# Attention weights times v: the first v tile loaded as 64 partitions of heads, and the next-to-last store cut into 112, 11 and 5 rows

## The chip, the core and the metric

The kernel runs on one core of a Trainium2 chip. The metric is the device time of one execution in microseconds (us). The kernel before was timed three times: 1051.83 us in the median, 1051.76 at the lowest and 1052.38 at the highest.

## What is computed

The reference is one contraction, for 8 batches of 12 heads. Inputs and output are float32.

```python
batch, n_heads, seq, head_dim = 8, 12, 1024, 64
# attn_weights: [8, 12, 1024, 1024], v: [8, 12, 1024, 64]
np.einsum('bhqs,bhsd->bhqd', attn_weights, v)
```

The weights are 402.65 MB, v and the output 25.17 MB each, so 453 MB have to cross between HBM and the core.

## The kernel before

**Tiles.** The 96 heads are taken four at a time: 24 groups q, each in two units n (48 units). A unit's weights are one transfer (`load_attn`, L346) of 128 partitions (four heads, 32 partitions each), 64 KB read and 32 KB written per partition, because this transfer also turns float32 into bf16. Two buffers `abf` take turns. The last two units are loaded in two halves each.

**Compute.** For each unit TensorE transposes the weights (L146); VectorE and ScalarE copy the result out of PSUM into `at` (L276). For the first unit of a group TensorE also spreads the group's v from `vr` over all partitions (L163) and two engines copy it to `vbf` (L252). Then it multiplies (L191). The product is copied to `ot` (L288), transposed back in the next unit (L176), and copied to `osb` (L259), the output buffer of ten slots. Each unit's transposes done, GpSimd (POOL) issues the load of the unit after next into the buffer that came free: the order on POOL is written out by hand in the loop `for n in range(NU - 2)`.

**v.** From group 2 on, v comes as bf16 through POOL's queue into `vr` (`load_v`, L352). The first two groups (8 heads) take another way. SyncE (SP) loads them as float32 into two slots of `osb` that are not yet used, called `v32` (128 partitions of 16 KB: 16 partitions per head, so partitions 0 to 63 hold group 0 and partitions 64 to 127 group 1). The 16 KB are loaded as two halves of the columns: the first 8 KB of all 128 partitions before the main section starts (L136, 1 MB), the second 8 KB as the first transfer in it (L413, 1 MB, `V_REST`). VectorE casts the first half to `vr` in two copies (L334), POOL the second (L393). `s_vr` tells TensorE that v is there: POOL's cast raises it by 2, for both groups, after waiting on `s_v0` for the second transfer and for VectorE's copies. The main section is entered by VectorE, ScalarE and SP once the first transfer has landed; POOL issues the first two weight loads ahead of that.

**Stores.** Outputs of groups 0 to 19 are stored by POOL's queue, in bursts of 2 to 8 groups (L360). The last four groups go by SP's queue: groups 20 and 21 in one transfer of 2 MB, group 22 in one of 1 MB (both through `store`, L360, behind SP's wait for the second half of the last weights, L430), and group 23 in one of 1 MB at the very end (L436). ScalarE waits for the three with `s_end`.

Two queues are told apart in the profile: q0, POOL's, with the weight loads, later v and most stores; and q1, SP's, with the first v and the last stores. Both feed the same 16 DMA engines; a transfer of 128 rows puts 8 rows on each.

Of the kernel before, what the change touches and what calls it, by code (L numbers as in the profile page):

```python
# [10 lines left out]
def kernel(  # L11
# [18 lines left out]
    nc = tc.nc  # L30
# [4 lines left out]
    B, H, Q, S = attn_weights.shape  # L35
    D = v.shape[-1]
    NH = B * H
    P = 128
# [4 lines left out]
    HP = P // 2  # L43
    KW = S // (2 * P)
    SB = S // P
    V8 = 2 * VH
    VB = S // (P // V8) // SB
    VR = 32
    NV = NH // VH
# [8 lines left out]
    V_SLOT = 4  # L58
    V_AT_ONCE = 4
    V_LOADS = {2: 2, **{q: V_AT_ONCE for q in range(V_AT_ONCE, NV, V_AT_ONCE)}}  # L60

    V_REST = ((0, P),)
    HALVED = NU - 2
    TOGETHER = 8
    BURSTS = {8: ((0, 8),), 16: ((8, 2), (10, 6))}
# [3 lines left out]
    def slot(q):  # L69
        return q % NO  # L70

    attn_q = attn_weights.rearrange("b (hq four) (p r) s -> (b hq) (four p) (r s)", four=VH, p=VP)
    out_q = out.rearrange("b (hq four) (p r) d -> (b hq) (four p) (r d)", four=VH, p=VP)
    out_h = out.rearrange("b h q d -> (b h) q d")

    def out_n(q, fours):
        return out_h[ds(q * VH, fours * VH)].rearrange(
            "(n four) (p r) d -> (four p) n (r d)", four=VH, p=VP
        )
# [3 lines left out]
    def v_n(q, fours):  # L83
        return v_h[ds(q * VH, fours * VH)].rearrange(
            "(n eight) (p r) d -> (eight p) n (r d)", eight=V8, p=P // V8
        )
# [17 lines left out]
    vr = sb("vr", [P, V_AT_ONCE // 2, VB, SB * D], bf16)  # L104
    vbf = sb("vbf", [P, SB, VH, D], bf16)
    ot = sb("ot", [P, GH, P], fp32)
    osb = sb("osb", [P, NO, 2 * G, D], fp32)

    v32 = osb[:, ds(V_SLOT, 2)].rearrange("p n r d -> p n (r d)")
    v_first = v_n(0, 2)[:, 0].rearrange("p (half x) -> p half x", half=2)  # L110
    vr_first = vr[:, 0].rearrange("p (half b) x -> p half (b x)", half=2)
    bank = [nc.alloc_psum_tensor(f"bank{i}", [P, 512], fp32).ap() for i in range(8)]
    pt = [b.rearrange("p (k j) -> p k j", k=KW) for b in bank[:4]]
    po = bank[4:6]
# [5 lines left out]
    s_v0, s_v = sem("s_v0"), sem("s_v")  # L120
    s_osb = sem("s_osb")
    s_held, s_end = sem("s_held"), sem("s_end")
# [8 lines left out]
    s_out, s_fin = sem("s_out"), sem("s_fin")  # L131
    s_const, s_vr = sem("s_const"), sem("s_vr")

    s_half, s_free = sem("s_half"), sem("s_free")

    nc.sync.dma_start(out=v32[:, 0], in_=v_first[:, 0])  # L136

    with tc.tile_critical(sync_engine=mybir.EngineType.Pool, no_gpsimd_drain=True):
        pe = nc.tensor
# [189 lines left out]

        for h in range(2):  # L330
            nc.vector.memset(ot[:, :, ds(h * HP, HP)], 0.0).then_inc(s_ot)
        for half in range(2):
            part = ds(half * (SB * D * VB // 4), SB * D * VB // 4)
            last = nc.vector.tensor_copy(out=vr_first[:, 0, part], in_=v32[:, 0, part])  # L334
        last.then_inc(s_v0)
        engine(True)
        engine(False)
        nc.scalar.wait_ge(s_held, 16 * (BY_SYNC - HELD_FROM) // 2)
# [2 lines left out]
        pool = nc.gpsimd  # L341

        def load_attn(n):
            pieces = [(0, G)] if n < HALVED else [(0, GH), (GH, GH)]
            for g0, gn in pieces:
                pool.dma_start(  # L346
                    out=abf[n % 2][:, ds(g0, gn)].rearrange("p g s -> p (g s)"),
                    in_=attn_q[n // 2][:, ds((n % 2 * G + g0) * S, gn * S)],
                ).then_inc(s_abf[n % 2] if g0 == 0 else s_second[n], 16)

        def load_v(q, fours):
            pool.dma_start(  # L352
                out=vr[:, ds(q % V_AT_ONCE // 2, fours // 2)].rearrange("p n b x -> p n (b x)"),
                in_=v_n(q, fours),
            ).then_inc(s_v, 16)

        def store(q, fours, eng, done):
            eng.wait_ge(s_out, 2 * (q + fours) + 1)
            at_slot = osb[:, ds(slot(q), fours)].rearrange("p n r d -> p n (r d)")
            eng.dma_start(  # L360
                out=out_n(q, fours), in_=at_slot,
                **({"single_packet": True} if eng is pool and fours == 2 else {}),
            ).then_inc(done, 16)

        def store_2(q):
# [7 lines left out]
            out=ident,  # L373
            in_=ident,
# [9 lines left out]
            out=spread,  # L384
            in_=spread,
# [3 lines left out]
            pattern=[[-P, V8], [-1, P + VB - 1]],  # L389
            channel_multiplier=VB,  # L390
        ).then_inc(s_const)
        pool.wait_ge(s_v0, 16 * len(V_REST) + 1)
        pool.tensor_copy(out=vr_first[:, 1], in_=v32[:, 1]).then_inc(s_vr, 2)  # L393
        for n in range(NU - 2):
            q, i = n // 2, n % 2
            if i == 0 and q + 1 in V_LOADS:
                pool.wait_ge(s_sp, 4 * (q + 1))
                load_v(q + 1, V_LOADS[q + 1])
            pool.wait_ge(s_t[True], (n + 1) * PER_DVE)
            load_attn(n + 2)  # L400
            if i == 0 and q % TOGETHER == 0 and 0 < q <= HELD_FROM:
                for q0, fours in BURSTS[q]:
                    store(q0, fours, pool, s_osb)
# [5 lines left out]

        for p0, pn in V_REST:
            nc.sync.dma_start(  # L413
                out=v32[ds(p0, pn), 1], in_=v_first[ds(p0, pn), 1]
            ).then_inc(s_v0, 16)
        nc.sync.sem_inc(s_free, NO // 2)
        nc.sync.sem_inc(s_half, WHOLE[0])
        for k in range(1, NV // 2):
# [9 lines left out]
        for n in range(HALVED, NU):  # L428
# [1 line left out]
            nc.sync.sem_inc(s_half)  # L430
        nc.sync.wait_ge(s_osb, 16 * sum(len(x) for x in BURSTS.values()))
        store(NV - 4, 2, nc.sync, s_end)
        store(NV - 2, 1, nc.sync, s_end)
        nc.sync.wait_ge(s_fin, 2)
        nc.sync.wait_ge(s_out, NU)
        nc.sync.dma_start(  # L436
            out=out_q[NV - 1], in_=osb[:, slot(NV - 1)].rearrange("p r d -> p (r d)")
        ).then_inc(s_end, 16)
        landed = nc.scalar.alloc_register("landed")
        nc.scalar.reg_mov(landed, 16 * 3)  # L440
    tc.keep_in_program_order(nc.scalar.wait_ge(s_end, nc.scalar.snap(landed)))
    tc.keep_in_program_order(nc.scalar.sem_inc(s_end, 1))

# [29 lines left out]
```

## Time and profile before

| | |
|---|---|
| time of the profiled execution | 1051.83 us |
| its span, first to last instruction | 1050.0 us |
| TensorE (PE) busy | 795.4 us, 76% of the span |
| VectorE (DVE) busy | 388.7 us, 37% |
| ScalarE (ACT) busy | 410.6 us, 39% |
| POOL busy | 39.1 us, 4% |
| moved in HBM | 427.82 MB read, 25.17 MB written |
| packets of q1 in the trace, 8,192 B each | 309 ns in the median |
| packets of a weight load on q0, 32,768 B written | 2,432 ns in the median |
| a weight load, from issue to landing | 29.2 us in the median |

The profile counts bytes of a DMA at its destination, so a weight load of 8 MB in HBM is 4,096 KB there. Its rate of 229 GB/s in the mean is therefore about half of what is read, while the last line of its third part gives the rate in HBM, 431 GB/s over the span. The line "DMA" of its second part is the busy share of the 16 DMA engines in 40 slices of the span. The trace also has a record of each packet that a DMA engine moved (start, length, size, queue); the same packets strung together by their ends give the work of each of the 16 engines. Times within the span are counted from its start.

### The profile page before, as it was taken

The numbers are of one execution on the slowest core, as the hardware profiler recorded it, in microseconds if no ns is written. First come the engines' busy times: TensorE is split into PE (matmuls) and PEld (weight loads), VectorE is DVE, ScalarE is ACT, GpSimd is POOL, SyncE is SP. The second block draws the span as 40 slices with busy tenths as digits, with TensorE's granted clock in tenths as the row PEclk, the third lists the DMA queues.
The fourth block names the chain that finished last, engine by engine and source line by source line (L and its number), as shares of the span: only waits on it lengthen the run. The fifth ranks groups of instructions, "written<-read, shape, count | busy, mean of one in ns | idle before, by whom it ended". The sixth has DMA issues, their size and how long they took to land.

```text
span 1050.0 us, 17183 instructions
## 1 busy us (share of the span) xinstructions
PE 795.4 (76%) x7304; PEld 708.4 (67%) x7304; DVE 388.7 (37%) x583; ACT 410.6 (39%) x493; POOL 39.1 (4%) x68
## 2 busy tenths in 40 slices
PE   0878789489789492887949779859568975887995
PEld 0777678478678482777848678647547865776885
DVE  1443344235334251343424344324223432453443
ACT  0444344335335251343425344334224433444443
POOL 1000000000000000000000000000000000000000
PEclk9989889799898796889879989889878988899898
DMA  9999999999999999999999999999999999999999
GB/s 232 229 218 219 217 216 212 217 220 218 217 218 216 212 216 379 217 218 217 207 218 220 220 218 217 207 224 212 324 275 217 218 206 220 217 220 220 209 218 352
DMA packets 12198, 240.20 MB, mean 229 GB/s; under 512 B 1056, under 2 KB 1056, under 8 KB 1056
## 3 DMA queue, kind: packets, MB, share of 16 engines
q0 software_dynamic: 11344, 233.84, 99.1%
q1 hardware_dynamic: 848, 6.29, 1.5%
q8 instruction: 3, 0.05, 0.0%
q14 instruction: 3, 0.02, 0.0%
HBM read 427.82 MB, written 25.17 MB: 431 GB/s over the span
## 4 chain that ended last, share of the span: by engine, by line
DMA 71%; PE 26%; issue 1%; POOL 0%; ACT 0%; DVE 0%; ACTq 0%; SPq 0%; POOLq 0%
DMA abf<-in_attn_weights_dram 63%; PE bank L146 22%; DMA out_dram<-osb 8%; PE bank L163 3%; PE bank L191 1%; PE bank L176 1%; POOL vr L352 0%; ACT vbf L252 0%; ACT osb L259 0%; DVE osb L259 0%; ACT ot L288 0%; POOL abf L346 0%; ACTq L259 0%; SPq L424 0%; SPq L423 0%
## 5 line engine op out<-in xcount | busy, mean ns | idle before, releaser
L146 PE MATMUL bank<-ident,abf 128*128 128x128 f32 x3072 | 430.0, 307 | 215.3 <-DMA abf<-in_attn_weights_dram 188.2
L146 PEld LDWEIGHTS bank<-ident,abf 128*128 128x128 f32 x3072 | 420.4, 212 | 227.1 <-DMA abf<-in_attn_weights_dram 195.6
L276 DVE COPY at<-bank 128x1024 bf16<-128x1024 bf16 x480 | 319.7, 689 | 405.1 <-PE bank L146 400.6
L276 ACT COPY at<-bank 128x1024 bf16<-128x1024 bf16 x288 | 287.9, 1012 | 332.0 <-PE bank L146 332.0
L191 PE MATMUL bank<-at,vbf 128*64 128x256 bf16 x3072 | 225.7, 285 | 0.0
L191 PEld LDWEIGHTS bank<-at,vbf 128*64 128x64 bf16 x3072 | 203.7, 111 | 19.4 <-issue 6.3
L288 DVE COPY ot<-bank 128x512 f32<-128x512 f32 x48 | 33.2, 692 | 208.6 <-PE bank L191 208.6
L288 ACT COPY ot<-bank 128x512 f32<-128x512 f32 x48 | 28.1, 585 | 185.9 <-PE bank L191 185.9
L163 PE MATMUL bank<-vr,spread 32*128 32x512 bf16 x768 | 87.0, 375 | 0.6 <-issue 0.2
L176 PE MATMUL bank<-ident,ot 128*128 128x128 f32 x392 | 62.4, 312 | 29.4 <-ACT vbf L252 28.7
L176 PEld LDWEIGHTS bank<-ident,ot 128*128 128x128 f32 x392 | 51.3, 159 | 41.4 <-ACT vbf L252 40.5
L259 ACT COPY osb<-bank 128x512 f32 (+1 forms) x97 | 53.4, 588 | 31.2 <-PE bank L176 29.3
L163 PEld LDWEIGHTS bank<-vr,spread 32*128 32x128 bf16 x768 | 35.2, 93 | 44.0 <-issue 1.7
L346 POOL DMA_DIRECT2D abf<-in_attn_weights_dram x50 | 26.9, 538 | 788.7 <-PE bank L146 787.7
L252 ACT CAST vbf<-bank 128x512 bf16<-128x512 f32 x48 | 25.8, 589 | 74.4 <-PE bank L163 74.4
L252 DVE CAST vbf<-bank 128x512 bf16<-128x512 f32 x48 | 30.9, 686 | 29.1 <-PE bank L163 29.1
L276 ACT ACT_TABLE_LOAD x12 | 15.4, 1283 | 6.7 <-DMA osb<-in_v_dram 6.5
L352 POOL DMA_DIRECT2D vr<-in_v_dram x6 | 4.0, 674 | 136.3 <-PE bank L163 136.3
L360 POOL DMA_DIRECT2D out_dram<-osb x5 | 3.9, 786 | 12.0 <-ACT osb L259 12.0
L393 POOL CAST vr<-osb 128x2048 bf16<-128x2048 f32 x1 | 1.9, 1889 | 22.0 <-DMA osb<-in_v_dram 22.0
L327 DVE MEMSET ident<- 128x128 f32 x1 | 0.2, 165 | 6.5 <-DMA osb<-in_v_dram 6.5
L334 DVE CAST vr<-osb 128x1024 bf16<-128x1024 f32 x2 | 2.2, 1138 | 0.0
(9 smaller groups left out, 5.3 us busy)
## 6 DMA issues: line engine op xcount, KB each, us to landing
abf<-in_attn_weights_dram POOLq DMA_DIRECT2D x46, 4096.0 KB, 29.2
vr<-in_v_dram POOLq DMA_DIRECT2D x5, 2048.0 KB, 15.3
out_dram<-osb POOLq DMA_DIRECT2D x1, 8192.0 KB, 41.7
abf<-in_attn_weights_dram POOLq DMA_DIRECT2D x4, 2048.0 KB, 23.0
out_dram<-osb POOLq DMA_DIRECT2D x3, 2048.0 KB, 33.4
out_dram<-osb POOLq DMA_DIRECT2D x1, 6144.0 KB, 41.7
osb<-in_v_dram SPq DMA_DIRECT2D x2, 1024.0 KB, 15.7
out_dram<-osb SPq DMA_DIRECT2D x1, 2048.0 KB, 14.4
```

Source lines behind the costliest of these rows:

```text
L146: last = pe.matmul(out=pt[g % 4][:, k], lhsT=words[:, k], rhs=ident, is_transpose=True, start=(k == 0), stop=(k == KW - 1),)
L163: last = pe.matmul(out=banks[h], lhsT=spread[rows, j, ds(VB - 1 - b, P)], rhs=vr[rows, n // 2, b], start=(b == 0), stop=(b == VB - 1),)
L176: last = pe.matmul(out=ps[:, ds(j * P, P)], lhsT=ot[:, j0 + j], rhs=ident, is_transpose=True, start=(j == 0), stop=(j == jn - 1),)
L191: last = pe.matmul(out=outs, lhsT=vbf[:, 2 * kw + par, h], rhs=at[:, ds(half * GH, GH), kw, ds(h * VP, VP), par], start=(n == 0), stop=(n ...
L252: copy(out=vbf[:, :, h], in_=ps.rearrange("p (k d) -> p k d", k=SB)).then_inc(s_vbf)
L259: return copy(out=rows.rearrange("p (half j) d -> p j half d", half=2)[:, ds(j0, jn)], in_=ps[:, ds(0, jn * P)].rearrange("p (j half d) -> ...
L276: ins = copy(out=at[:, g].rearrange("c k j two -> c (k j two)"), in_=bank[g % 4].bitcast(bf16),)
L288: copy(out=ot.rearrange("c j (h p) -> c h j p", h=VH)[:, ds(2 * e, 2)], in_=po[e].rearrange("c (h j p) -> c h j p", h=2, j=GH),).then_inc( ...
L334: last = nc.vector.tensor_copy(out=vr_first[:, 0, part], in_=v32[:, 0, part])
L346: pool.dma_start(out=abf[n % 2][:, ds(g0, gn)].rearrange("p g s -> p (g s)"), in_=attn_q[n // 2][:, ds((n % 2 * G + g0) * S, gn * S)],).th ...
L352: pool.dma_start(out=vr[:, ds(q % V_AT_ONCE // 2, fours // 2)].rearrange("p n b x -> p n (b x)"), in_=v_n(q, fours),).then_inc(s_v, 16)
L360: eng.dma_start(out=out_n(q, fours), in_=at_slot, **({"single_packet": True} if eng is pool and fours == 2 else {}),).then_inc(done, 16)
```

## The change

The first two groups' v is now split by partitions and not by columns. What is loaded before the main section is group 0 alone: partitions 0 to 63, 16 KB each, as two transfers of 64 x 8 KB (0.5 MB each). Group 1 (partitions 64 to 127) follows as one transfer of 64 x 16 KB in place of L413. VectorE casts group 0 in two copies of 64 x 2,048 elements and raises `s_vr` itself; POOL casts group 1 in one copy of 64 x 4,096 elements, and does so behind the issue of unit 2's weight load, no longer ahead of the loop. On SP the store of group 22 becomes three transfers, of rows 0 to 111, 112 to 122 and 123 to 127; ScalarE's last wait counts two transfers more. All bytes moved are the same as before.

```diff
-    V_REST = ((0, P),)
+    UNEVEN = ((0, 112), (112, 11), (123, 5))
...
+    four = [ds(0, HP), ds(HP, HP)]
+    VC = S * V8 * D // P // 2
+    part = [ds(0, VC), ds(VC, VC)]
...
-    nc.sync.dma_start(out=v32[:, 0], in_=v_first[:, 0])
+    for x in part:
+        nc.sync.dma_start(out=v32[four[0], x], in_=v_first[four[0], x])
...
-        for half in range(2):
-            part = ds(half * (SB * D * VB // 4), SB * D * VB // 4)
-            last = nc.vector.tensor_copy(out=vr_first[:, 0, part], in_=v32[:, 0, part])
-        last.then_inc(s_v0)
+        for x in part:
+            last = nc.vector.tensor_copy(out=vr_first[four[0], x], in_=v32[four[0], x])
+        last.then_inc(s_vr)
...
-        pool.wait_ge(s_v0, 16 * len(V_REST) + 1)
-        pool.tensor_copy(out=vr_first[:, 1], in_=v32[:, 1]).then_inc(s_vr, 2)
         for n in range(NU - 2):
...
             load_attn(n + 2)
+            if n == 0:
+                pool.wait_ge(s_v0, 16)
+                pool.tensor_copy(out=vr_first[four[1]], in_=v32[four[1]]).then_inc(s_vr)
...
-        for p0, pn in V_REST:
-            nc.sync.dma_start(
-                out=v32[ds(p0, pn), 1], in_=v_first[ds(p0, pn), 1]
-            ).then_inc(s_v0, 16)
+        nc.sync.dma_start(out=v32[four[1]], in_=v_first[four[1]]).then_inc(s_v0, 16)
...
-        store(NV - 2, 1, nc.sync, s_end)
+        nc.sync.wait_ge(s_out, 2 * (NV - 1) + 1)
+        for p0, pn in UNEVEN:
+            nc.sync.dma_start(
+                out=out_q[NV - 2, ds(p0, pn)],
+                in_=osb[ds(p0, pn), slot(NV - 2)].rearrange("p r d -> p (r d)"),
+            ).then_inc(s_end, 16)
...
-        nc.scalar.reg_mov(landed, 16 * 3)
+        nc.scalar.reg_mov(landed, 16 * (2 + len(UNEVEN)))
```

More of the change, by code (lines that the diff above doesn't have):

```diff
@@ L107 @@
     osb = sb("osb", [P, NO, 2 * G, D], fp32)
-    v32 = osb[:, ds(V_SLOT, 2)].rearrange("p n r d -> p n (r d)")
-    v_first = v_n(0, 2)[:, 0].rearrange("p (half x) -> p half x", half=2)
-    vr_first = vr[:, 0].rearrange("p (half b) x -> p half (b x)", half=2)
+    v32 = osb[:, ds(V_SLOT, 2)].rearrange("p n r d -> p (n r d)")
+    v_first = v_n(0, 2)[:, 0]
+    vr_first = vr[:, 0].rearrange("p b x -> p (b x)")
+    four = [ds(0, HP), ds(HP, HP)]
+    VC = S * V8 * D // P // 2
+    part = [ds(0, VC), ds(VC, VC)]
     bank = [nc.alloc_psum_tensor(f"bank{i}", [P, 512], fp32).ap() for i in range(8)]
```

## The prediction

> **What bounds the kernel now.** I read the page's parts 2 and 3 first. The line "DMA" is full in all 40 slices, and one queue alone fills 99.1% of the 16 DMA engines' time:
>
> ```profile
> span 1050.0 us, 17183 instructions
> ...
> PE 795.4 (76%) x7304; PEld 708.4 (67%) x7304; DVE 388.7 (37%) x583; ACT 410.6 (39%) x493; POOL 39.1 (4%) x68
> ...
> DMA  9999999999999999999999999999999999999999
> ...
> q0 software_dynamic: 11344, 233.84, 99.1%
> q1 hardware_dynamic: 848, 6.29, 1.5%
> ```
>
> TensorE, the busiest engine, works 76%. The chain of waits agrees: 71% of it is DMA, and its pieces alternate between a weight load's transfer and the 64 transposes that free the buffer for the load after next. Then the packet records: strung together, they give 16 DMA engines that carry packets from 1.85 us on, with no gap of 0.5 us or more on any, until they end between 1047.5 and 1048.7 us; the instructions end 1.3 us later. So the time is a sum of packets, and the engine with the longest sum ends it. No wait between compute engines matters unless it leaves a DMA engine without packets, and a loss on a DMA engine passes to the end in full. Two loads are always under way: when one's successor is issued, the other load still has about half of its 8 x 2.43 = 19.5 us of packets to run. The sum is made against the profiled execution, 1051.83 us, which is also the median of the three runs (span 1050.0 and 1.83 us around it).
>
> The start, from the timeline:
>
> ```profile
> 0.74 0.38 SPq L136 DMA_DIRECT2D osb<-in_v_dram  x1
> 1.34 1.23 POOL L346 DMA_DIRECT2D abf<-in_attn_weights_dram  x2 [0.90 <-POOLq L457]
> 6.33 0.33 SPq L413 DMA_DIRECT2D osb<-in_v_dram  x1
> ...
> 8.77 2.19 DVE L334 CAST vr<-osb 128x1024 bf16<-128x1024 f32 x2
> 27.68 9.12 PEld L146 LDWEIGHTS bank<-ident,abf 128*128 128x128 f32 x64 [27.68 <-DMA abf<-in_attn_weights_dram]
> ...
> 32.41 1.89 POOL L393 CAST vr<-osb 128x2048 bf16<-128x2048 f32 x1 [22.00 <-DMA osb<-in_v_dram]
> ```
>
> The reader is to see that the first transfer of v is ahead of everything on the DMA engines, and that the compute engines have nothing to do before 27.68 us but small preparations.
>
> **Casts: 0.** VectorE's two copies double in elements per partition: 2 x 2.19 = 4.4 us for 2.19, done by about 15.5 us even when they start 2 us later; VectorE's next work waits for the transposes at 27.68 us. POOL's cast likewise grows from 1.89 to 3.8 us, and stands behind the issue of unit 2's load (37.30 us). What is queued behind it is the issue of unit 3's load, 35 us later; the next to need its data is TensorE's spread at 77.11 us. `s_vr` for group 0 comes at 15.5 instead of 34.3 us, where TensorE uses it at 37.23 us: the wait there was not binding. If the cover were gone, VectorE's 2.2 us would only move copies of unit 0, which sets no DMA engine idle.
>
> **The first v: +2.05 us.** Before, each of the 16 engines moves 8 packets of 8,192 B. All but the first packets take 309 ns, one every 306; the first take 316 to 1,685. The engines finish between 4.79 and 5.83 us, in the mean at 5.05, and on all 16 the first load packet starts 5 to 6 ns behind the last record of v. The loads wait behind v on each engine. The number of bytes stays. But they now land in 64 partitions, 16 x 8,192 B per 306 ns, or 428 GB/s, into half as many rows. The trace shows no such transfer. The ends: nothing, if the 306 ns are the engine's own; or 8 x 309 ns = 2.47 us, if 64 partitions take only half of what 128 do. I take the ceiling that has been seen: 428 GB/s for 128 partitions, thus 214 GB/s for 64. It is the fastest that any partition receives in this trace; the weight loads write half as fast (32,768 B in 2,432 ns). Then 1,048,576 B take 4.90 us; from about 2.2 us, when the first packets are through, that ends at 7.1, against 5.05 in the mean: +2.05 us (part of the slow first packets is hidden, since engines that share rows wait for one another anyway).
>
> [...]
>
> **The second v: +0.8 us.** Before, its 8 packets of 322 ns per engine take turns with load packets of 2.43 us. After, 4 packets of 16,384 B do. At the engines' pace they take 4 x 0.62 us, the same work. Bounds: 0, and 4 x 0.62 = 2.48 us if each packet takes double. On average the upper 64 partitions need, per turn of 2.43 + 0.62 = 3.05 us, 8 x 32,768 B of load and 16 x 16,384 B of v, 172 GB/s, which is below the 214. So only coincidences cost: an engine that sends v to rows that another is filling with weights. I take a third of the upper end, 0.8 us. If the ceiling doesn't exist, this is 0.
>
> **The cut store: 0, bounds -0.31 and +0.31 us.** The 16 engines end at 1047.47 to 1047.98 us (eleven) and at 1048.24 to 1048.72 (five). With 112 rows as 7 on each engine, 11 rows on eleven and 5 on five, five engines carry 9 rows, six 8 and five 7, where all had 8; a packet is 306 ns. If the five late ones are the relieved, the end moves to 1048.41, -0.31; if one of the late is among the five with 9, +0.31. The records don't say which engine is which, so I take 0. The two more issues on SP (0.45 us each by the first two, 0.96 us in all for two) end by 1031.4 us; engines take up q1 at 1033.07 or later, and SP's next issue is at 1041.34 us.
>
> ```profile
> 1029.49 0.96 SPq L360 DMA_DIRECT2D out_dram<-osb  x2
> ...
> 1041.34 0.33 SPq L436 DMA_DIRECT2D out_dram<-osb  x1
> ```
>
> **Sum.** 1051.83 + 2.05 + 0.8 + 0 = 1054.7 us.
>
> **Rivals.**
> 1. *No ceiling in the partitions; not slower.* 64 partitions take 428 GB/s. Decided by the pace of a v packet in the first 6 us: 309 ns, and not near 618. For it: the engines move about 8 KB in 304 to 309 ns whether they write 8 KB into the core, 4 KB (cast loads) or read from it, as if the limit were in the engine. Against: no partition has been seen to take more than in that transfer. Then only the cut store is left: 1051.8 us, 1051.4 to 1052.2.
> 2. *Load packets fill the gaps.* If an engine takes a load packet in between as soon as POOL's descriptors are there, the slow v costs only until then: about half of 2.05, 1052.8 us, with some of the second v 1053.3. For it: later the two queues do take turns, packet by packet (10 to 32 us, and again from 1033 us). Against: at the start none of the 16 engines did; all 8 v packets went ahead, though the loads were issued at 1.34 us.
> 3. *The second v collides fully.* 2.05 + 2.48: 1056.4 us. For it: half the engines send into rows that others fill, and the last engine ends the kernel. Against: the mean need of 172 GB/s fits.
> 4. *The 11 and 5 rows all go to one engine.* It would carry 7 + 16 = 23 rows instead of 8: 15 x 0.306 = 4.6 us, if everything else is nothing 1056.4 us. Nothing in the trace has an odd number of rows. [...]
>
> **How the numbers follow.** Forecast (first v at half pace, second partly) 0.42, with its own range 1053.6 to 1055.7; rival 1 0.27; rival 2 0.13; rival 3 0.12; rival 4 0.04; something that saves over 2.1 us 0.02, for which I find no source: the engines' ends lie 1.25 us apart, and that is all that better balance could give. The range 1051.5 to 1056.3 leaves out the lowest part of rival 1, about half of rivals 3 and 4, and the last case, some 0.15 together. What a measurement of this kernel can tell from no change is about 0.2%, 2.1 us: slower means above 1053.9. That takes nine tenths of the forecast, rivals 3 and 4 and a little of rival 2: 0.56. Within: 0.42. Faster: 0.02.
>
> **What would show it.** In the profile after: the first v lands at about 8 us instead of 6.2 (SP's second issue moves from 6.33 to about 8.3 us), its packets last near 618 ns, and the first load packets start near 7 us. The second v's packets last 0.62 us without collisions and up to 1.24 with. PE's first transposes move from 27.68 to about 30 us, and everything behind them by the same 2 to 3 us up to the last store's issue, 1041.34 us before. In the tail the engines carry 7, 8 or 9 rows of group 22. If v's first packets still take 309 ns, the main step is wrong and rival 1 holds; if load packets lie between them, rival 2; if one engine ends some 4 us behind the others, rival 4.

## The result and the profile after

The changed kernel takes 1055.44 us in the median of 8 runs (1053.92 to 1059.22), the kernel before 1051.85 (1051.73 to 1052.38): a ratio of 1.0038, 95% interval 1.0028 to 1.0047. It is slower by 3.6 us, clear of what the measurement can tell, and its executions differ from one another by 5 us where those of before differ by 0.7. The profiled execution took 1056.10 us (span 1054.3). The forecast was 1054.7 us, slower, with 1051.5 to 1056.3 as the range; the time lies inside it, but two of the terms that it was added up from were far off, as the parts below show.

Parts 1 to 3 of the page after, the span and the queues (packets, MB, share of the time of 16 DMA engines):

```profile
span 1054.3 us, 17185 instructions
...
DMA  9999999999999999999999999999999999999998
...
q0 software_dynamic: 11344, 233.84, 98.7%
q1 hardware_dynamic: 816, 6.29, 1.7%
```

The DMA engines are as full as before. q1 moves the same 6.29 MB, but its packets take 1.7% of the engines' time and not 1.5%, and that of a longer span; by the packet records 18.4 us per engine instead of 15.5. The work of the engines has become longer, with the same bytes.

The timeline of the start (start, busy us, engine and line, and in brackets the idle time before it and what ended it), and behind it how long the two transfers of group 0 took from issue to landing:

```profile
0.74 1.18 SPq L140 DMA_DIRECT2D osb<-in_v_dram  x2
1.34 1.24 POOL L349 DMA_DIRECT2D abf<-in_attn_weights_dram  x2 [0.90 <-POOLq L463]
19.07 0.47 SPq L416 DMA_DIRECT2D osb<-in_v_dram  x1
19.22 0.17 DVE L331 MEMSET ident<- 128x128 f32 x1 [19.22 <-DMA osb<-in_v_dram]
...
21.52 3.25 DVE L337 CAST vr<-osb 64x2048 bf16<-64x2048 f32 x2
29.18 10.10 PEld L150 LDWEIGHTS bank<-ident,abf 128*128 128x128 f32 x64 [29.18 <-DMA abf<-in_attn_weights_dram]
...
39.77 0.57 POOL L349 DMA_DIRECT2D abf<-in_attn_weights_dram  x1 [16.08 <-PE bank L150]
40.39 3.59 POOL L404 CAST vr<-osb 64x4096 bf16<-64x4096 f32 x1
...
L140 SPq DMA_DIRECT2D osb<-in_v_dram x2: 549/562/575, 0.7 to 1.3; - x2
...
DMA to landing us min/median/max: 5.5/11.5/17.5
```

Three things are to be seen. The main section is entered at 19 us, not at 6.3: the second of the two transfers of group 0, issued at 1.3 us, takes 17.5 us to land. TensorE starts at 29.18 us, 1.5 later than before. And the casts still have cover: VectorE's end at 24.8 us, ahead of the spread (L167) at 39.71, and POOL's at 44.0, ahead of the next group's spread at 81.12.

The packet records say where the 1.5 us come from, and that it doesn't end there. One DMA engine of each kernel (start in us, 0.05 more here than counted from the first instruction; packet lengths in ns; v packets of 8 KB, or 16 KB where marked):

```
before  v 1.85+864, then seven of 309; load 4.85+2431, 7.26+2432, 9.68+2435; v 12.09+322; load 12.41+2431; ...
after   v 2.15+820 2.97+311 3.27+618 3.88+654; load 4.52+2526; v 7.03+322; load 7.35+2431; v 9.76+322; ...
        v 25.19+1052 (16 KB) 26.24+1649 (16 KB); load 27.88+2431; v 30.29+1058 (16 KB); load 31.32+2492;
        v 33.79+1064 (16 KB); ...
```

The records don't name their engine; which packets stand on the same one is inferred from starts that meet ends. All 16 engines together, in us per engine beyond the regular length (306 ns per 8 KB of v, 2,432 per load packet):

```
                              before   after   difference
first v, start of first packet  2.08    2.35     0.27
first v, packets too long       0.51    1.11     0.60
second v, packets too long      0.12    2.26     2.14
load packets beside them        0.04    0.50     0.46
sum                                              3.47
second load lands, mean        46.39   49.81     3.42
second load lands, last engine 47.46   51.91     4.45
last packet, last engine     1048.72 1053.02     4.30
```

From the second load's landing to the last weight load the mean delay stays between 3.2 and 3.5 us: nothing is lost or regained in 980 us, and what the start lost arrives at the end. The table is of one execution, which took 1056.10 us and is one of the longer ones. At the tail SP's issues moved by 4.4 us:

```profile
1033.85 0.42 SPq L363 DMA_DIRECT2D out_dram<-osb  x1
1034.33 2.21 SPq L436 DMA_DIRECT2D out_dram<-osb  x3
1045.71 0.36 SPq L442 DMA_DIRECT2D out_dram<-osb  x1
```

### The profile page after: what moved, and what is told of

It is laid out like the page before. It is cut to its first block, busy times and chain, and to the rows that moved or that the text cites. A ratio compares the mean times of both kernels' runs of the same rounds, so it can differ in the third digit from the quotient of the medians.

```text
span 1054.3 us, 17185 instructions
## 1 busy us (share of the span) xinstructions
PE 794.3 (75%) x7304; PEld 708.1 (67%) x7304; DVE 389.9 (37%) x583; ACT 410.6 (39%) x493; POOL 41.4 (4%) x68
## 3 DMA queue, kind: packets, MB, share of 16 engines
q1 hardware_dynamic: 816, 6.29, 1.7%
## 4 chain that ended last, share of the span: by engine, by line
DMA 71%; PE 26%; issue 1%; POOL 0%; ACT 0%; DVE 0%; ACTq 0%; SPq 0%; POOLq 0%
DMA abf<-in_attn_weights_dram 63%; PE bank L150 22%; DMA out_dram<-osb 8%; PE bank L167 3%; PE bank L195 1%; PE bank L180 1%; POOL vr L355 0%; ACT vbf L256 0%; ACT osb L263 0%; DVE osb L263 0%; ACT ot L292 0%; POOL abf L349 0%; ACTq L263 0%; SPq L425 0%; SPq L424 0%
## 5 line engine op out<-in xcount | busy, mean ns | idle before, releaser
L167 PE MATMUL bank<-vr,spread 32*128 32x512 bf16 x768 | 87.0, 375 | 0.5 <-issue 0.2
L167 PEld LDWEIGHTS bank<-vr,spread 32*128 32x128 bf16 x768 | 35.0, 93 | 44.1 <-issue 1.7
L404 POOL CAST vr<-osb 64x4096 bf16<-64x4096 f32 x1 | 3.6, 3591 | 0.1
L337 DVE CAST vr<-osb 64x2048 bf16<-64x2048 f32 x2 | 3.2, 1662 | 0.0
```

The source lines that it names most:

```text
L167: last = pe.matmul(out=banks[h], lhsT=spread[rows, j, ds(VB - 1 - b, P)], rhs=vr[rows, n // 2, b], start=(b == 0), stop=(b == VB - 1),)
L404: pool.tensor_copy(out=vr_first[four[1]], in_=v32[four[1]]).then_inc(s_vr)
```

## The experiments

Theories are named in the expectations as they stood: **A**, engines that write v into 64 partitions at once get half the rate, in the second v above all; **B**, packets of 16 KB are what is slow; **C**, the cut store costs a good part; later **A2**, below.

**1. The cut store alone**, in the kernel before.

```diff
+    UNEVEN = ((0, 112), (112, 11), (123, 5))
...
-        store(NV - 2, 1, nc.sync, s_end)
+        nc.sync.wait_ge(s_out, 2 * (NV - 1) + 1)
+        for p0, pn in UNEVEN:
+            nc.sync.dma_start(out=out_q[NV - 2, ds(p0, pn)], in_=...).then_inc(s_end, 16)
...
-        nc.scalar.reg_mov(landed, 16 * 3)
+        nc.scalar.reg_mov(landed, 16 * (2 + len(UNEVEN)))
```

> The kernel before with the cut store alone (112, 11 and 5 rows). Theory A (the loss comes at the start, from engines that write v into 64 partitions): 1051.85 us within 0.31 either way, since a row is 306 ns; the engines end 7, 8 and 9 rows later than where they would, nothing else moves. Theory C (the cut store costs a good part of it, since one engine is left with more): 1053 us or more, with one group of engines ending over 1 us after the others. If the 11 and 5 rows all fall on one engine: 1056 us.

1052.36 us (before 1051.84; ratio 1.0007, 0.9998 to 1.0016), with two executions of eleven at 1054.19 and 1055.06. C falls as the main cause: about 0.5 us, which the interval doesn't tell from none. But four packets of the cut store last 533 to 1,019 ns; the store whole, in the kernel before and in experiment 2, shows none above 352.

**2. The v edits alone**: the changed kernel with that store whole.

```diff
-        for p0, pn in UNEVEN:
...
+        store(NV - 2, 1, nc.sync, s_end)
...
```

> The changed kernel with group 22's store whole again, so the v edits alone. Theory A: 1055.2 us (1054.5 to 1056), almost all of the change's loss, and the same wide spread between executions as the changed kernel had. Theory C: 1053.5 us or less.

1054.70 us (before 1051.84; ratio 1.0028, 1.0017 to 1.0039), executions from 1053.51 to 1056.20: 2.9 of the 3.6 us and a spread of 2.7 us are there without the cut store. The profiled execution is the shortest of the eight.

**3. The second v by rows, packets of 8 KB**, in the kernel before.

```diff
-    V_REST = ((0, P),)
+    V_REST = ((0, HP), (HP, HP))
```

> The kernel before, with its second transfer of v (128 partitions of 8 KB) cut into two transfers of 64 partitions of 8 KB; the first transfer and the store as before. Theory A (16 engines writing to the rows that half of them are filling with weights): the packets last well over 322 ns, 500 to 600 in the mean, and the kernel takes 1053.5 to 1055 us. Theory B (the packets of 16 KB are what is slow in turns with loads): packets of 8 KB stay at 322 ns, 1051.9 us.

1052.06 us (before 1051.84; ratio 1.0001, 0.9992 to 1.0010). The packets last 331 ns in the mean, nearly all 322; only where a second v packet follows the first without a load packet in between, 376 to 462. So 64 rows as such don't cost: theory A falls in the form in which I had put it, and B is ahead.

**4. Group 1 by POOL's queue**, with the cast on the way (16 KB read, 8 KB written per packet), in the changed kernel with the store whole.

```diff
         load_attn(1)
+        pool.dma_start(out=vr_first[four[1]], in_=v_first[four[1]]).then_inc(s_v0, 16)
...
-        nc.sync.dma_start(out=v32[four[1]], in_=v_first[four[1]]).then_inc(s_v0, 16)
+        nc.sync.wait_ge(s_v0, 16)
+        nc.sync.sem_inc(s_vr, 1)
...
-            if n == 0:
-                pool.wait_ge(s_v0, 16)
-                pool.tensor_copy(out=vr_first[four[1]], in_=v32[four[1]]).then_inc(s_vr)
...
```

> The changed kernel with the store whole, and group 1's v (64 partitions) loaded by POOL's queue behind the first two weight loads, cast on the way to bf16, so that 16 KB are read and 8 KB written per packet; SP's second transfer and POOL's cast are gone. Theory A: 16 engines write into 64 rows at half their rate, which the rows can take: packets of about 608 ns, 1052.7 us (only the first v's loss is left). Theory D (any transfer into 64 partitions loses, whatever it writes): packets near 1,200 ns and 1055 us.

1052.66 us (before 1051.84; ratio 1.0008, 0.9999 to 1.0017), and its 64-row packets last 628 ns in the mean (POOL's other packets of this size: 625). Here an engine's four packets follow one another, with no load packet between: 16 x 8,192 B per 625 ns, or 210 GB/s into the 64 rows. What is left, 0.8 us (interval -0.1 to +1.8), is put down to the first v. Two of the 2.9 us came with the second v's own form.

**5. Packets of 16 KB into all rows.** After experiment 3 the question was B against **A2**, a supposition: half the rows take half the rate, but one packet of 8 KB can be held back and written under the next load packet, which writes at half the engines' pace (32,768 B in 2,432 ns, where v has 8,192 B in 309); 16 KB don't fit.

```diff
-                out=v32[ds(p0, pn), 1], in_=v_first[ds(p0, pn), 1]
+                out=v32_all[ds(p0, pn)], in_=v_n(0, 2)[:, 0][ds(p0, pn)]
...
```

(`v32_all` is two other slots, 6 and 7; POOL casts the second half from there.)

> The kernel before, with its second transfer of v made as wide as 128 partitions of 16 KB (both halves, 2 MB, into two other slots that are free then), so packets of 16 KB into all partitions; 1 MB is loaded twice. The extra MB alone is 8 x 0.306 = 2.45 us. Theory A2 (half the rows take half the rate, but an engine can hold back about one packet of 8 KB and write it under the next load packet; 16 KB into half the rows do not fit): into all rows the 8 packets last 620 ns each, 1054.3 us. Theory B (packets of 16 KB in turns with loads are slow wherever they go): packets of 1,000 ns or more, 1057 us or more.

1054.30 us (before 1051.95; ratio 1.0022, 1.0013 to 1.0031), +2.35 where the extra MB alone makes 2.45, executions within 0.5 us. All 128 packets last 611 to 631 ns. B falls: packets of 16 KB in turns with loads are not slow as such. Of this kernel's part 3:

```profile
q1 hardware_dynamic: 848, 7.34, 1.7%
```

It moves 1.05 MB more than the changed kernel on q1, in the same 1.7%.

**6. The second v into 64 rows, but by 8 KB**, in the changed kernel with the store whole.

```diff
-        nc.sync.dma_start(out=v32[four[1]], in_=v_first[four[1]]).then_inc(s_v0, 16)
+        for x in part:
+            nc.sync.dma_start(out=v32[four[1], x], in_=v_first[four[1], x]).then_inc(s_v0, 16)
...
-                pool.wait_ge(s_v0, 16)
+                pool.wait_ge(s_v0, 32)
...
```

> The changed kernel with the store whole and group 1's v as two transfers of 64 x 8 KB in place of one of 64 x 16 KB. Theories A2 and B alike: single packets of 8 KB in turns with loads stay near 322 ns, except where two follow each other; 1052.7 us, the first v's loss alone. If it is 64 rows as such, whatever the packet (theory A as first put): 1054.7 us as with the store whole.

1053.26 us (before 1051.95; ratio 1.0012, 1.0003 to 1.0021): 1.4 us less than with 16 KB, though 0.6 more than expected. The packets last 342 ns in the mean, 322 in the median, up to 573 where two follow each other. Also when many engines send v at once they mostly stay short: the 21 packets beside which on average at least nine other engines were sending v last 322 ns in the median and 390 in the mean. Neither the rows alone (3: 331 ns per 8 KB in the mean) nor the packet alone (5: 611 to 631 ns per 16 KB) costs much; 16 KB into 64 rows does (872 ns in the mean in experiment 2).

**7. The first v in two transfers, but by columns**, in the kernel before.

```diff
-    nc.sync.dma_start(out=v32[:, 0], in_=v_first[:, 0])
+    for c0 in (0, 1024):
+        nc.sync.dma_start(out=v32[:, 0, ds(c0, 1024)], in_=v_first[:, 0, ds(c0, 1024)])
```

> The kernel before, with its first transfer of v cut into two of 128 partitions x 4 KB. It tells whether the first v's loss (0.8 us in the kernel with group 1 by POOL) is from 64 rows or from being two transfers. Rows: packets of about 155 ns, 1051.9 to 1052.1 us. Two transfers (a later start, a second issue): 1052.6 us.

1052.36 us (before 1051.95; ratio 1.0003, 0.9994 to 1.0012). Between the two answers: packets of 159 ns in the median, so no half pace, but 0.4 us all the same. All 16 v packets of each engine, those of both transfers, stand ahead of its first load packet. With 0.8 in experiment 4, two transfers and 64 rows may share it; the intervals are too wide to divide it further.

**8. The second half of the columns by POOL's queue**, in the kernel before, as a possible better version.

```diff
         load_attn(0)
+        pool.dma_start(out=vr_first[:, 1], in_=v_first[:, 1]).then_inc(s_v0, 16)
         load_attn(1)
...
```

> The kernel before, with the second half of v's columns loaded by POOL's queue behind the first weight load, cast to bf16 on the way, for all 128 partitions; SP's second transfer and POOL's cast are gone. It reads the same bytes; 8 KB take 304 ns there against 322 on SP's queue, so 8 x 18 ns = 0.14 us less: 1051.7 us, which is the same as before. If the turns between the queues cost more than the packets show: up to 0.5 us faster.

1051.78 us (before 1051.95; ratio 0.9999, 0.9990 to 1.0008). As expected, and the same as before.

**9. All of the first v by POOL's queue**, in the kernel before, nothing by SP.

```diff
-    nc.sync.dma_start(out=v32[:, 0], in_=v_first[:, 0])
...
         load_attn(0)
+        pool.dma_start(out=vr[:, ds(0, 1)].rearrange("p n b x -> p n (b x)"), in_=v_n(0, 2)).then_inc(s_v0, 16)
         load_attn(1)
...
```

> The kernel before, with all of the first v loaded by POOL's queue behind the first weight load, cast to bf16, 128 partitions of 16 KB; SP loads nothing and neither VectorE nor POOL casts. It shows when the first load packet can start if no v is ahead of it. If at about 2 us: the slow first packets (0.5 us per engine in the mean) fall on the load, 1051.4 to 1051.8 us. If only at 3 us or later: the engines stand idle for 1 us, 1052.5 us or more.

1052.88 us (before 1051.86; ratio 1.0008, 0.9999 to 1.0017). The first load packets start at 2.96 us in the mean (2.77 at the earliest), some 0.8 later than v's in the kernel before. So loads are there at about 2.8 us, and in the kernel before they stood behind v until 4.8 to 5.8. That is what rival 2 had left open.

**10. The cut made even**: 112 and 16 rows, in the kernel before. The edit is shown against experiment 1.

```diff
-    UNEVEN = ((0, 112), (112, 11), (123, 5))
+    UNEVEN = ((0, 112), (112, 16))
```

> The kernel before, with group 22's store cut into 112 and 16 rows, so that each engine carries 7 + 1 = 8 rows. The cut into 112, 11 and 5 alone had taken 1052.36 us, and its only slow packets (533 to 1,019 ns) were of the small transfers, one row per engine. Theory A2 (engines that work on few neighbouring rows at once share what these rows can give): the 16 rows are slow in the same way, several packets of 500 to 1,000 ns, 1052.2 to 1052.6 us. If it is the unequal number of rows: no slow packets, 1051.9 us.

1051.89 us (before 1051.86; ratio 1.0002, 0.9993 to 1.0011), and no packet above 352 ns in the profiled execution. That speaks against few neighbouring rows as the cause, as far as one execution can. But two of eleven executions took 1053.22 and 1054.16 us.

**11. The same even cut in the changed kernel.**

```diff
-    UNEVEN = ((0, 112), (112, 11), (123, 5))
+    UNEVEN = ((0, 112), (112, 16))
```

> The changed kernel with group 22's store cut into 112 and 16 rows, 8 on each engine. With the store whole it took 1054.70 us, with 112, 11 and 5 rows 1055.44. If the unequal rows make the 0.7 us: 1054.7 us. If the cut as such does: 1055.3 us. In the profile the second v's 64 packets of 16 KB are slow again (870 ns and 1,180 ns in the mean in two executions so far), and the more so the later the last weight load lands: the end follows them one for one.

1055.74 us (before 1051.91; ratio 1.0039, 1.0027 to 1.0051; 1053.99 to 1057.93). It is no faster than with unequal rows, but six executions that spread over 4 us can't tell 0.7. The profile gives a third execution of the slow second v:

```
                      packets of 16 KB, mean   last engine's third load lands   last packet   time
before                          -                     66.86 us                    1048.72      1051.83
store whole                  872 ns                   68.56                       1050.42      1053.51
cut 112 and 16               991                      69.97                       1051.99      1055.12
changed kernel             1,178                      71.23                       1053.02      1056.10
```

The order is the same in all columns: the longer the second v's packets last in an execution, the longer it takes. That this makes the spread rests on these three executions. The table also says what the tail adds: the last packet is as late as the third load was (4.30 us against 4.37 in the changed kernel, 3.27 against 3.11 with 112 and 16 rows, 1.70 both times with the store whole). In the changed kernel's profiled execution the cut store thus costs nothing at the end.

**12. Small transfers first**: 5, 11, 112 rows, in the kernel before. The edit is shown against experiment 1.

```diff
-    UNEVEN = ((0, 112), (112, 11), (123, 5))
+    UNEVEN = ((0, 5), (5, 11), (16, 112))
```

> The kernel before with group 22's store cut into 5, 11 and 112 rows, the small transfers first (rows 0 to 4, 5 to 15, 16 to 127), so that they are carried while POOL's queue still takes turns. If what was slow in the kernel with 112, 11 and 5 rows (533 to 1,019 ns) is a single row read at the same time as other single rows with nothing in between: the small transfers now last 309 ns, 1051.9 us. If it is the two small transfers by themselves: slow packets again, about 1,040 us into the span, and 1052.4 us.

1052.26 us (before 1051.91; ratio 1.0006, 0.9997 to 1.0014). Slow packets again (365 to 826 ns), but at 1044.7 to 1046.8 us, in the 112 rows and not in the small transfers. Neither answer holds. The profiled execution is one of the longer ones, 1053.47 us; 1.0 of its 1.6 us more is there when its last whole weight load lands (991.4 against 990.4 us), ahead of the store.

## Why the prediction was right, and where it was not

- **What bounds the kernel**: right. From the second load on the mean delay never falls below 3.2 us, and of the 4.45 us on the last engine 4.30 are there at the last packet.
- **Casts at 0**: right. VectorE's took 3.25 us (4.4 expected), POOL's 3.59 (3.8). The cover shrank more than foreseen, since the section was entered at 19 and not near 8 us; 4.4 us of it were left.
- **"The first v: +2.05 us"**: the step that failed by size. The half pace is there: the last v packet ahead of the loads takes 639 to 665 ns on 14 of the 16 engines, and 16 x 8,192 B in 650 ns are 202 GB/s, close to the 214 of the estimate. That engines which share rows wait for one another was the author's estimate too; no record shows it. But the price fell on about four packets per engine, not eight. The term had assumed that loads wait behind all of v. They did so in the kernel before, where one transfer brings the eight packets (first load packets at 4.8 to 5.8 us); of the second transfer here most packets took turns with loads, at 322 ns. That is rival 2, for half of the first v. So the first load packets came at 4.2 to 5.2 us and not near 7, and SP's second issue at 19.07 and not at 8.3. Why the second transfer didn't go ahead as well is not shown; it is issued at 1.35 us, just behind POOL's first load (1.34), while in experiment 7, where both transfers went ahead, the second is issued at 1.18. Measured: 0.27 + 0.60 = 0.87 us in the profile, 0.8 in experiment 4.
- **"The second v: +0.8 us ... only coincidences cost"**: the step that failed the other way. By the medians of experiments 2 and 4 it is 2.0 us. In the profiled execution it is 2.14 + 0.46 = 2.6 us per engine, near the 2.48 of rival 3 (a little of the 0.46 stands beside the first v). I had divided the need evenly over 3.05 us. But 14 of 16 engines begin their first 16 KB packet between 24.9 and 25.7 us, and send 256 KB at once into 64 rows, where the 64 rows of the first v took 202 GB/s. The mean need (172 GB/s) fits, the need of the moment doesn't. That explains a part: the 22 packets beside which on average at least eleven other engines were sending v last 1,472 ns in the mean, but the other 42 still last 1,024, and not 624. The size of the packet decides, which the prediction didn't ask: with 8 KB into the same rows it is 0.2 to 0.5 us (experiments 3 and 6).
- **The sum**: it came near by luck. In the medians the v edits cost 2.9 us, and the forecast had 2.85; but the first term was 1.2 too large and the second 1.2 too small. Half the rate into half the rows fits the first v (202 GB/s, against 428 into 128 rows before); of the second it explains only a part.
- **The cut store: 0**: small, as said, and its size is open. In the kernel before it is +0.5 us, with an interval from -0.2 to +1.7. Between the medians of the changed kernel and experiment 2 lie 0.7, but their executions spread over 5.3 and 2.7 us, and in the changed kernel's trace the tail adds nothing to what the start lost (experiment 11). So the 0.7 are not shown to be the cut's. The bounds counted rows. The engines carry 7, 8 or 9 of them as foreseen (rows between semaphore writes: 7; 7 and 1; 7, 1 and 1), so rival 4 falls. What the bounds left out are single slow packets in the cut transfers, up to 1,019 ns. I could not settle their cause: neither single rows (10, 12) nor the unequal rows (11) account for all of them. SP's three issues took 2.21 us, not 3 x 0.45; they still ended 9 us ahead of the next.
- **Rival 1** fell: 64 partitions didn't take 428 GB/s. The most that was seen where the 16 engines' packets follow one another is 210 (experiment 4).

That an engine holds back about one packet of 8 KB is an estimate from packet lengths (322 ns alone, up to 573 in pairs, 640 in a row, 870 to 1,180 for 16 KB); no record shows such a store. What makes packets of 16 KB into 64 rows slow in turns with loads, when each alone is not, thus stays open. No version here is faster than the kernel before.

## What to carry to other kernels

In this kernel the DMA engines never pause, and what lengthened their packets at the start passed to the end: 4.45 us on the last engine when the second load lands, 4.30 at the last packet, although TensorE was busy for 75% of the span only. So ask first whether the DMA engines of a kernel pause. The second v's mean need, 172 GB/s by the prediction's estimate, was below the 202 that 64 rows took, and its packets were still 2.14 us per engine too long: 14 of 16 engines began them within 0.8 us of one another, which explains a part. So price a transfer into half of the partitions by the need of the moment too, and ask how large its packets are: in turns with loads 8 KB lasted 331 to 342 ns in the mean into 64 rows, and 16 KB 872 to 1,178. A forecast that comes out near can still rest on two terms that cancel: check the terms, not only the sum.

## What was not expected of the hardware

- 16 KB packets into 64 partitions in turns with loads lasted 872 to 1,178 ns in the mean of three executions, and 622 into 128 partitions; 8 KB packets 331 to 342 in the mean into 64 and 320 into 128. Load packets beside the first kind also grew, from 2,432 up to 3,173 ns in the changed kernel.
- Eight packets of a transfer went ahead of load packets that were ready (2.8 us, experiment 9) for 2 to 3 us; with two transfers of four only the first four or five did, and with two transfers by columns all sixteen (experiment 7).
- Executions spread over 2.7 us with such a transfer (experiment 2) and over 3.2 with the cut store alone (experiment 1), over 5.3 with both (the changed kernel), where 16 KB into all rows stayed within 0.5.
